# A two-block transformer kernel: the experts' rare branch moved into the last pair, pooling's weights through the chunk ring, sparse attention's keys projected first

## The chip, the cores and the metric

The kernel runs on one core of a Trainium2 chip. A core has five engines, each with its own instruction queue: TensorE (PE, matrix products; its weight loads are listed apart as PEld), VectorE (DVE), ScalarE (ACT), GpSimd (POOL) and SyncE (SP, which here only issues DMAs). They wait for one another on semaphores. The metric is the device time of one execution in microseconds, as the median of the runs.

## The reference

The input is x[256, 1024] in float32. The first block modulates and normalises x, mixes tokens by three branches (attention, gated linear attention, a long convolution), and adds a mixture of 16 experts of which each token takes two from one group. The second block has two layers. Each is a feed-forward, a mixer and another feed-forward, all with norms before and after:

```python
def grouped_moe(h, router_w, router_b, w_gate, w_up, w_down):
    scores = sigmoid(h @ router_w)                    # 16 experts in 4 groups
    sel = scores + router_b
    group = argmax(sum of the 2 best sel in each group)
    idx = top_k(sel inside the group, 2); w = scores[idx] / sum
    for e in range(16):                               # gates: w, or 0
        out += gates[:, e] * ((silu(h @ w_gate[e]) * (h @ w_up[e])) @ w_down[e])

def second_block(x, g, ...):
    for i in range(2):
        x = x + 0.5 * rms_norm(swiglu(rms_norm(x, g[i, 0]), ...), g[i, 1])
        h = rms_norm(x, g[i, 2])
        m = pool_mixer(h) if i == 0 else nsa_mixer(h)
        x = x + rms_norm(m, g[i, 3])
        x = x + 0.5 * rms_norm(swiglu(rms_norm(x, g[i, 4]), ...), g[i, 5])

def pool_mixer(h, w_grp, b_grp, scale):   # 4 channel groups, windows 2, 4, 8, 16
    d = trailing mean over the window - h             # per group
    return (d @ w_grp[g] + b_grp[g]) * scale

def nsa_mixer(h, ...):
    q, k_c, v_c, k_s, v_s, k_w, v_w, gate = split(h @ w_in)
    # compressed keys and values: blocks of 32 tokens through silu(z @ w1) @ w2
    o = sig(gate)[0] * o_compressed + sig(gate)[1] * o_selected + sig(gate)[2] * o_window
    return o @ w_o
```

## The kernel before, in words

Activations stay in on-chip memory, 256 tokens as two tiles `t` of 128 rows. Weights are streamed from memory in chunks of up to 1 MB, requested by SP (L120) into a ring of buffers `wr`; a request waits until the buffer's last reader is done. A float32 weight is split into a rounded part `wh` (ACT, L158) and a rest `wl` (DVE, L159), and a product is made of three passes of matmuls (L169, L171, L173).

*Router and experts* (`moe`). Logits (L992), the norm's sums (L229, L232), scores per token by a small transposing product (L1009), sigmoid, then a chain of small DVE instructions picks group and experts (L1038 to L1064), while PE transposes the tokens (L1027). The tokens are split into `th` and `tl` by ACT (L1031, L1032) and POOL (L1033). `places` writes a 0/1 matrix `put` that gathers up to 64 tokens (`CAP`) of four experts at a time into `xg` by a product (L1092). `fill` (L222) is a matmul without a use for its result. Experts go in eight pairs of 12 chunks each. `first(q)` makes gate and up of pair q (L1138), in its middle the hidden part of the pair before is finished; `second` and `finish` of the pair before (L1184, L1185) follow. The chunk ring has 13 buffers here. If an expert has more than 64 tokens, a branch (L1217) computes the overflow expert by expert; in this input none has, and each engine jumps over some 1500 rows of its program. The branch stands behind the last pair.

*Second block* (`Second`). `ffn` streams 22 + 12 chunks, `project` makes the output, `add` normalises it and adds it to x, one token tile after the other; `after` transposes the next input. `E.ahead` splits the next feed-forward's first chunk early, by ACT (L137) and POOL (L138).

*Pooling* (`pool`). The weights come through the ring, the 1 MB of `band` (the windows' means as matrices), the bias and the scale by POOL's own requests when the stage begins (L84, L1734). For each tile: products (L1745), a scaled copy `v` by ACT (L1747), bias (L1752) and bands (L1754), a multiplication by `scale` (L1756), output.

*Sparse attention* (`nsa`). The columns are projected in the order k_c, v_c, q, k_s, k_w, gate, each 128 columns by three passes. `query` and `key` rotate (L1820, L1822 to L1824) and split by ACT and DVE. `compress` makes the compressed keys and values in steps between the projections. The gates take a sigmoid (L1940) and a transpose (L1945). Then `compressed(t)` makes the scores and probabilities of the compressed keys (L1956 to L1974), and 24 units of `scores` (L1991, L1995, L1997), `softmax` (L2004 to L2011) and `values` (L2022 to L2042) follow, the values two steps behind the scores.

The order on each engine is set by a scheduler that follows the order of the code and its dependences; `issue_after` holds an instruction behind another one.

Of the kernel before, what the change touches and what calls it, by code (L numbers as in the profile page):

```python
# [17 lines left out]
D = 1024  # L18
# [19 lines left out]
class Env:  # L38


    def __init__(self, ctx, tc, W):
        self.ctx = ctx
        self.begun = None
        self.rings = []
        self.beside = ExitStack()
# [56 lines left out]
    @contextmanager  # L102
    def ring(self, name, n):

        with self.pool(name) as p:
            yield p, n

    @contextmanager
    def more_ring(self, n):

        with self.ring("ringmore", n) as r:
            self.rings = [r, *self.kept]
            self.wn = (2048, *self.wn[1:])
            self.turn = 0
            yield
        self.rings = self.kept[:1]
# [6 lines left out]
    def load(self, src, n, eng=None):  # L123

        places = [r for r in self.rings for _ in range(r[1])]
# [3 lines left out]
    def ahead(self, src, n):  # L129
# [4 lines left out]
        with self.tc.high_priority():  # L134
            for i in range(0, n, 512):
                j = slice(i, i + 512)
                ins = self.nc.scalar.activation(hi[:, j], raw[:, j], AF.Copy).ins  # L137
                self.nc.gpsimd.tensor_sub(lo[:, j], raw[:, j], hi[:, j].bitcast(F32))  # L138
        return (hi, lo), ins
# [17 lines left out]
    def split(self, hi, lo, src, eng=None):  # L157
        self.nc.scalar.activation(hi, src, AF.Copy)  # L158
        (eng or self.nc.vector).tensor_sub(lo, src, hi.bitcast(F32))  # L159
# [182 lines left out]
def packs(np, x):  # L342
# [60 lines left out]
    d["rows"] = np.stack([np.broadcast_to(r, (128, 1024)) for r in (g[0, 1], g[0, 3], g[0, 5], g[1, 1], g[1, 3], g[1, 5], x["pool_scale_2"].reshape(1024))])  # L403
    d["pool_b"] = x["pool_b_2"].reshape(1, 1024)
# [5 lines left out]
    cols = np.concatenate([k_c, v_c, q, k_s, k_w, gate, np.zeros((1024, 208), np.float32)], 1)  # L410
# [523 lines left out]
class Chunks:  # L934
# [25 lines left out]

    def take(self):
        return self.got.pop(0) if self.got else self.E.load(next(self.todo), 2048)


def moe(E, W, VI, mc, router, tiles, chunks, xT):
# [18 lines left out]
    def scaled():  # L984

        for k in tiles:
# [5 lines left out]
            mm = PE.matmul(lg[32 * j : 32 * j + 32, :T], rw[:, k], xa[:, k], start=k < 4, stop=k >= 4)  # L992
            if k == KD - 1:
                E.fill(mm.ins, 6)
# [5 lines left out]
    more = es.enter_context(ExitStack())  # L1000
    more.enter_context(E.more_ring(6))
# [6 lines left out]
    for t in range(2):  # L1008
        PE.matmul(lt[:, 16 * t : 16 * t + 16], ls[:, 128 * t : 128 * t + 128], E.sel[:, :16], start=True, stop=True)  # L1009
# [12 lines left out]
    V.tensor_tensor(sel, scores, rb.unsqueeze(1).to_broadcast([128, 2, 16]), OP.add)  # L1022
    for c in range(2):
# [446 lines left out]
class Second:  # L1470
# [94 lines left out]
    def project(self, units, xs, kt, up, after, behind=(), between=None):  # L1565
# [5 lines left out]
        def product(t, w, h, k0, n):  # L1571
# [4 lines left out]
            if k0 + n == kt:  # L1576
                self.out_half(t, h, bank[h, t], self.rows)
                if h:
                    self.add(t, up, after)
# [560 lines left out]
```

## Time and profile before

| | |
|---|---|
| runs | 1717.15 us median of 3 (1712.97 to 1720.77) |
| profiled execution | 1721.04 us, span 1719.3 us, mean granted clock 0.975 |
| busy share of the span | PE 96%, DVE 58%, ACT 45%, POOL 8% |
| DMA | 343.39 MB, mean 200 GB/s over the span |

The busy share is a mean over stages. The windows of the trace give, for a stretch, the busy time of each engine, the TensorE clock that was granted (1.00 is 2.4 GHz, 0.50 is 1.2 GHz) and the DMA share. The timeline lists instructions by start; in brackets stands how long the engine had been idle and what ended that.

### The profile page before, as it was taken

To read this page: it belongs to the slowest core of one execution; us is meant where nothing else is said; L and a number is where in the kernel's file an instruction comes from. 1 tells how busy PE (TensorE), PEld (TensorE's weight loads), DVE (VectorE), ACT (ScalarE), POOL (GpSimd) and SP (SyncE) were. 2 spreads that over 40 slices of the span, in tenths; PEclk is the share of its full clock that TensorE was granted. 3 is DMA by queue.
4 is the path that set the end of the run, shared out by engine and by line. 5 is a ranking of instruction groups with operands and counts; after the bars stand their busy time and mean duration, and the time that the engine had idled before them with its cause. 6 is when DMAs were issued, how large, how long until landed. Compare 5 with 4: busy or idle time off the path is not lost.

```text
span 1719.3 us, 24121 instructions
## 1 busy us (share of the span) xinstructions
PE 1651.5 (96%) x9266; PEld 1286.0 (75%) x9266; DVE 998.1 (58%) x2034; ACT 775.6 (45%) x1616; POOL 145.4 (8%) x149
## 2 busy tenths in 40 slices
PE   6999898899989999989999999999999998999998
PEld 3777787799975444358888688888888897788886
DVE  4635869786552323156654666547555686885544
ACT  3533344365441001045544555436554575865442
POOL 1001215111120000020000000000000022300000
PEclk8999998999999999999999899999999998999999
DMA  9454353137537999956454454555455351065450
GB/s 361 165 185 164 126 169 124 62 99 296 182 145 309 426 425 426 426 227 225 171 188 167 176 190 165 187 193 205 176 182 184 137 198 58 22 257 200 169 190 33
DMA packets 60380, 343.39 MB, mean 200 GB/s; under 512 B 7329, under 2 KB 8161, under 8 KB 28769
## 3 DMA queue, kind: packets, MB, share of 16 engines
q1 hardware_dynamic: 57680, 333.29, 52.0%
q0 software_dynamic: 1776, 6.56, 1.1%
q10 hardware_dynamic: 800, 1.92, 0.3%
q8 instruction: 75, 1.23, 0.3%
q14 instruction: 49, 0.39, 0.1%
HBM read 340.69 MB, written 1.05 MB: 199 GB/s over the span
## 4 chain that ended last, share of the span: by engine, by line
PE 53%; DVE 1%; ACT 1%; DMA 0%; POOL 0%; issue 0%; DVEq 0%; POOLq 0%; ACTq 0%
PE mm L169 16%; PE mm L171 15%; PE mm L173 15%; PE mx L1658 1%; PE mx L1995 1%; PE mx L1507 1%; PE acc L2042 1%; PE mm L2022 1%; PE mm L1754 0%; DMA c_pool_b<-in_pool_b_dram 0%; PE mm L1752 0%; PE mm L1745 0%; PE acc L2031 0%; PE mx L1820 0%; PE acc L2035 0%
## 5 line engine op out<-in xcount | busy, mean ns | idle before, releaser
L159 DVE TENSOR_TENSOR wl<-wr,wh 128x512 fp32r<-128x512 f32 x768 | 498.4, 700 | 237.9 <-ACT wh L158 224.5
L158 ACT ACTIVATE wh<-wr 128x512 fp32r<-128x512 f32 x768 | 428.6, 622 | 307.2 <-PE mm L173 183.1
L169 PE MATMUL mm<-wh,xh 128*128 128x512 f32 (+1 forms) x752 | 204.0, 393 | 0.0
L173 PE MATMUL mm<-wh,xl 128*128 128x512 f32 (+1 forms) x752 | 198.6, 386 | 0.0
L171 PE MATMUL mm<-wl,xh 128*128 128x512 f32 (+1 forms) x752 | 198.2, 386 | 0.0
L173 PEld LDWEIGHTS mm<-wh,xl 128*128 128x128 f32 x752 | 139.1, 188 | 28.7
L171 PEld LDWEIGHTS mm<-wl,xh 128*128 128x128 f32 x752 | 139.1, 188 | 28.6
L169 PEld LDWEIGHTS mm<-wh,xh 128*128 128x128 f32 x752 | 136.1, 188 | 26.1 <-ACT xh L1519 0.4
L1138 PE MATMUL mm<-wr,xg 128*64 128x512 f32 x512 | 124.9, 596 | 0.0
L171 PE MATMUL mm<-wl,hidh 128*128 128x512 f32 x352 | 98.6, 396 | 0.0
L173 PE MATMUL mm<-wh,hidl 128*128 128x512 f32 x352 | 98.0, 396 | 0.0
L169 PE MATMUL mm<-wh,hidh 128*128 128x512 f32 x352 | 97.7, 395 | 0.0
L1650 DVE SCALAR_TENSOR_TENSOR L<-mm,r,L 128x256 f32<-128x256 f32 x88 | 42.5, 483 | 92.8 <-ACT L L1649 90.3
L1649 ACT ACTIVATE L<-mm,r 128x256 f32<-128x256 f32 x88 | 41.8, 475 | 117.5 <-PE mm L173 115.1
L1138 PEld LDWEIGHTS mm<-wr,xg 128*64 128x64 f32 x512 | 37.4, 137 | 67.3 <-issue 64.6
L173 PEld LDWEIGHTS mm<-wh,hidl 128*128 128x128 f32 x352 | 66.1, 188 | 15.8
L171 PEld LDWEIGHTS mm<-wl,hidh 128*128 128x128 f32 x352 | 65.9, 188 | 15.9
L169 PEld LDWEIGHTS mm<-wh,hidh 128*128 128x128 f32 x352 | 65.8, 188 | 15.6
L169 PE MATMUL mm<-hh,wh 128*128 128x256 f32 x480 | 75.1, 295 | 0.0
L173 PE MATMUL mm<-hh,wl 128*128 128x256 f32 x480 | 71.5, 288 | 0.0
L169 PEld LDWEIGHTS mm<-hh,wh 128*128 128x128 f32 x480 | 65.3, 195 | 7.7 <-issue 3.3
L171 PE MATMUL mm<-hl,wh 128*128 128x256 f32 x480 | 70.6, 287 | 0.0
(589 smaller groups left out, 2370.7 us busy)
## 6 DMA issues: line engine op xcount, KB each, us to landing
wr<-in_ffn_in_dram SPq DMA_DIRECT2D x88, 1024.0 KB, 4.8
wr<-in_moe_in_dram SPq DMA_DIRECT2D x64, 1024.0 KB, 12.7
wr<-in_ffn_out_dram SPq DMA_DIRECT2D x40, 1024.0 KB, 4.9
wr<-in_moe_out_dram SPq DMA_DIRECT2D x32, 1024.0 KB, 15.1
wr<-in_w_in_f_dram SPq DMA_DIRECT2D x55, 512.0 KB, 4.1
wr<-in_w_mod_dram SPq DMA_DIRECT2D x48, 512.0 KB, 6.1
wr<-in_nsa_in_f_dram SPq DMA_DIRECT2D x8, 1024.0 KB, 4.7
wr<-in_w_br_att_dram SPq DMA_DIRECT2D x8, 512.0 KB, 3.2
```

The source lines that it names most:

```text
L158: self.nc.scalar.activation(hi, src, AF.Copy)
L159: (eng or self.nc.vector).tensor_sub(lo, src, hi.bitcast(F32))
L169: nc.tensor.matmul(ps, lhs[0][k], rhs[0][k], start=first and k == 0, stop=False)
L171: nc.tensor.matmul(ps, lhs[0][k], rhs[1][k], start=False, stop=False)
L173: mm = nc.tensor.matmul(ps, lhs[1][k], rhs[0][k], start=False, stop=last and k == kt - 1)
L1138: PE.matmul(ps[s], x[:, s], w, start=start, stop=stop)
L1507: E.nc.tensor.transpose(tp[:, 128 * j : 128 * j + 128], self.x[:, t, c : c + 128], E.ident)
L1649: A(s, ps[:, :T], AF.Silu, scale=r)
L1650: V.scalar_tensor_tensor(h, ps[:, T:], r, s, OP.mult, OP.mult)
L1658: PE.transpose(tp[:, 256 * j + 128 * t : 256 * j + 128 * t + 128], hs[n, t][:, 128 * j : 128 * j + 128], E.ident)
L1995: PE.matmul(dst, qs[:, h // 2, h % 2, q], part[:, h // 4, :, : n // 2], start=t == 1 and i == 0, stop=t == 0 and i == 1 and j == 1)
L2022: PE.transpose(tp[:, 128 * j : 128 * j + 128], probs(u)[:, 128 * j : 128 * j + 128], E.ident)
```

## The change

Four places are rewritten.

1. *Router.* The six `fill` matmuls move behind the small transposing product. `th` is written by ACT straight from the transposes in PSUM, `tl` by DVE from there, two instructions behind the chosen mask (`rest_of(0, chosen)`), two behind the first `put`. POOL's subtractions go.
2. *Experts.* The ring has 16 buffers (7 + 2 on top of the kept 7); `xg` has one buffer instead of two. The branch stands in the last pair, after `first(7)`, once all chunks are requested (`chunks.fetch(8)`). The next feed-forward's first chunk is split behind the last pair's own split, and three more of its chunks are requested ahead (`E.queued`).
3. *Pooling.* Weights, rows and band come through the ring; the scale is folded into the weights and the bias by DVE; the bias is one product of one row and 512 columns per bank; the first tile's products and bands come before the feed-forward's add of the second tile (`half`). The next feed-forward's first three chunks are split behind that add (`behind`).
4. *Sparse attention.* Column order k_c, v_c, k_s, k_w, gate, q. The gate is 1 / (1 + exp(-z)) from the transposed values. Two units' scores come before the last query's rotation and the compressed scores; the compressed values' product moves to the end of each group of six units.

```diff
-    more.enter_context(E.more_ring(6))
+    E.more_ring(upper.enter_context(E.ring("ringtop", 2, "right")), more.enter_context(E.ring("ringmore", 7)))
...
-        PE.matmul(lt[:, 16 * t : 16 * t + 16], ls[:, 128 * t : 128 * t + 128], E.sel[:, :16], start=True, stop=True)
+        mm = PE.matmul(lt[:, 16 * t : 16 * t + 16], ls[:, 128 * t : 128 * t + 128], E.sel[:, :16], start=True, stop=True)
+    E.fill(mm.ins, 6)
...
             with E.tc.issue_after(scored):
-                A(h, tp, AF.Copy, scale=rt[:, t : t + 1])
-            nc.scalar.copy(th[:, t, q], h)
-            G.tensor_sub(tl[:, t, q], h, th[:, t, q].bitcast(F32))
+                A(th[:, t, 512 * c : 512 * c + 512], tp, AF.Copy, scale=rt[:, t : t + 1])
+
+    def rest_of(c, after):
+
+        with E.tc.issue_after(after.ins):
+            for t in range(2):
+                q = slice(512 * c, 512 * c + 512)
+                V.scalar_tensor_tensor(tl[:, t, q], turned[c, t], rt[:, t : t + 1], th[:, t, q].bitcast(F32), OP.mult, OP.subtract)
...
-        xg = gp.t([128, KD, n], "xg", 2)
+        xg = gp.t([128, KD, n], "xg")
...
         ps = first(xg[:, :, 128 * (q % 2) : 128 * (q % 2) + 128], two, lambda: next(late, None))
+        if q == 7:
+
+            chunks.fetch(8)
+            far = "far"
+            beyond()
+            far = ""
...
-    *_, last = late
-    E.fill(last, 4)
+
+    upper.close()
+    E.rings = E.kept[:1]
+    begun = E.ahead(W["ffn_in"][0, 0], 2048, done)
+    E.queued = [E.load(W["ffn_in"][0, u], 2048) for u in range(1, 4)]
+    for _ in late:
+        pass
     more.close()
...
-            band = E.const("pool_band", p)
-            b = E.const("pool_b", p)
-            scale = p.t([128, D], "scale")
-            nc.gpsimd.dma_start(scale, W["rows"][6])
+        w = E.load(W["pool_w"], 2048)
+        rows = E.load(W["pool_rows"], 2048)
+        band = E.load(W["pool_band"], 2048).rearrange("a (i g t) -> a i g t", i=2, g=4)
...
-            return tuple([a[:, 512 * k : 512 * k + 512] for k in range(4)] for a in E.wsplit(src[u], 2048))
+            return tuple([a[:, 512 * k : 512 * k + 512] for k in range(4)] for a in E.wsplit(src[u], 2048, behind=behind if u < 3 else ()))
...
-    cols = np.concatenate([k_c, v_c, q, k_s, k_w, gate, np.zeros((1024, 208), np.float32)], 1)
+    cols = np.concatenate([k_c, v_c, k_s, k_w, gate, np.zeros((1024, 208), np.float32), q], 1)
...
+                    A(g2, tp[:, :96], AF.Exp, scale=-1.0)
+                    V.tensor_scalar(g2, g2, 1.0, None, OP.add)
+                    V.reciprocal(g2, g2)
...
+            begin()
+            begin()
+            query(3)
             next(steps[0])
             next(steps[1])
-            next(steps[0])
-            begin()
-            begin()
```

PE around the branch, before: the last pair's `finish` (L1184, L1185), the fill, the branch, and behind its body the next feed-forward (L1674).

```order
L1184 MATMUL mx_6662<-back_6525,xa_6629 128x256
L1185 MATMUL mx_6662<-back_6525,xa_6629 128x256
L222 MATMUL mx_6666<-identr_73 128x512 x4
L1216 TENSOR_LOAD mosti_5425
L1217 COMPARE_AND_BRANCH
```

```order
L1217 UNCONDITIONAL_BRANCH x2
L229 MATMUL mx_11417<-ones_63,eps_69 128x2
L1674 MATMUL mm_11343<-hi_6677,xh_11319 128x512
L1674 MATMUL mm_11344<-hi_6677,xh_11319 128x512
L1674 MATMUL mm_11343<-lo_6678,xh_11319 128x512
```

The same engine now, ahead of the body and behind it (L1157 is the experts' product, L1141 and L1143 belong to `back`).

```order
L1157 MATMUL mm_6456<-wr_6503,xg_6214 64x512
L1157 MATMUL mm_6456<-wr_6505,xg_6214 64x512
L1218 TENSOR_LOAD mosti_5420
L1220 COMPARE_AND_BRANCH
L1141 MATMUL mx_6551<-c_start_61,putfar_6548 128x128 x2
```

```order
L1220 UNCONDITIONAL_BRANCH x2
L1141 MATMUL mx_11154<-c_start_61,put_6211 128x128 x2
L1143 MATMUL mx_11154<-r_812_5412,put_6211 128x2 x2
L1157 MATMUL mx_11164<-wr_6515,L_1039_6489 64x512
L1157 MATMUL mx_11164<-wr_6517,L_1039_6489 64x512
```

The branch has moved from between `finish` of the last pair and the next stage to between `first(7)` and `back(7)` with `second(6)`.

DVE at the pooling, before: the norm of the feed-forward's second tile from the output half (L1563) to its add (L1551), with the next feed-forward's weight splits (L159) between its steps.

```order
L1563 TENSOR_TENSOR xT_12368<-mm_12599,row_11450 128x512
L1498 TENSOR_SCALAR m_2270_12840<-ss_11322 128x1
L159 TENSOR_TENSOR wl_13143<-wr_13141,wh_13144 128x512
L196 TENSOR_SCALAR ny_2271_12842<-m_2270_12840 128x1
L159 TENSOR_TENSOR wl_13143<-wr_13141,wh_13144 128x512
L197 TENSOR_TENSOR nt_2272_12843<-ny_2271_12842 128x1
L159 TENSOR_TENSOR wl_13246<-wr_13244,wh_13247 128x512
L198 SCALAR_TENSOR_TENSOR nt_2272_12843<-nt_2272_12843,m_2270_12840 128x1
L159 TENSOR_TENSOR wl_13246<-wr_13244,wh_13247 128x512
L199 SCALAR_TENSOR_TENSOR nu_2273_12844<-nt_2272_12843 128x1
L159 TENSOR_TENSOR wl_13246<-wr_13244,wh_13247 128x512
L200 SCALAR_TENSOR_TENSOR nt_2272_12843<-nt_2272_12843 128x1
```

The same now (L1593 output half, L1581 add, L158 weight split).

```order
L1593 TENSOR_TENSOR xT_12359<-mm_12590,row_11445 128x512
L1528 TENSOR_SCALAR m_2273_12862<-ss_11319 128x1
L195 TENSOR_SCALAR ny_2274_12864<-m_2273_12862 128x1
L196 TENSOR_TENSOR nt_2275_12865<-ny_2274_12864 128x1
L197 SCALAR_TENSOR_TENSOR nt_2275_12865<-nt_2275_12865,m_2273_12862 128x1
L198 SCALAR_TENSOR_TENSOR nu_2276_12866<-nt_2275_12865 128x1
L199 SCALAR_TENSOR_TENSOR nt_2275_12865<-nt_2275_12865 128x1
L200 SCALAR_TENSOR_TENSOR nu_2276_12866<-nu_2276_12866,ny_2274_12864 128x1
L202 SCALAR_TENSOR_TENSOR rf_11323<-nt_2275_12865,nu_2276_12866 128x1
L1581 SCALAR_TENSOR_TENSOR x_11318<-xT_12359,rf_11323,x_11318 128x512 x2
L158 TENSOR_TENSOR wl_13094<-wr_13092,wh_13095 128x512 x3
```

Between the output half and the add no split is left; the first one stands behind the add.

PE at the start of the sparse attention, before: the last projection (L173, the gates), a rotation, the gates' transposes (L1945), the compressed scores (L1956, L1958), their transposes (L1974), and then the first unit's scores.

```order
L173 MATMUL mm_17082<-xh_11319,wl_17076 128x256 x8
L1820 MATMUL mx_17111<-L_2860_16990,c_nsa_rot_13092 128x512
L1945 MATMUL mx_17126<-c_start_61,L_2873_17107 128x48 x2
L1956 MATMUL mx_17134<-r_cmp_mask_13108,identr_73 128x256
L1958 MATMUL mx_17134<-kc_16425,xT_12368 128x32 x8
L1956 MATMUL mx_17154<-r_cmp_mask_13108,identr_73 128x256
L1958 MATMUL mx_17154<-kc_16425,xT_12368 128x32 x8
L1974 MATMUL mx_17174<-c_start_61,c_r_17152 128x128 x2
L1991 MATMUL mx_17178<-r_causal_13106,identr_73 128x512
```

The same engine now, from the second unit's scores (L2035) on: the last rotation (L1860), the compressed scores (L1996, L1998), and the transposes of the first two units' probabilities (L2062), with the compressed ones (L2014) behind the values (L2073).

```order
L2035 MATMUL mx_17110<-kh_16404,qs_16399 128x256
L2035 MATMUL mx_17110<-kl_16405,qs_16399 128x256
L1860 MATMUL mx_17126<-xT_12359,c_nsa_rot_13067 128x512
L1996 MATMUL mx_17138<-r_cmp_mask_13083,identr_73 128x256
L1998 MATMUL mx_17138<-kc_16400,xT_12359 128x32 x8
L1996 MATMUL mx_17158<-r_cmp_mask_13083,identr_73 128x256
L1998 MATMUL mx_17158<-kc_16400,xT_12359 128x32 x8
L2062 MATMUL mm_17231<-c_start_61,two_17094 128x128 x4
L2062 MATMUL mm_17238<-c_start_61,two_17094 128x128 x4
```

Scores of two units have moved ahead of the compressed scores, and the gates' transposes away from the end of the projections.

## Rows read from the trace of the kernel before

**Rows 1.** windows: length, busy PE, loads, DVE, ACT, POOL; clock, DMA share, GB/s

```profile
500.00:520.00 20.00, 13.14 (x74) 10.67 (x73) 10.58 (x40) 5.79 (x12) 4.95 (x4) 0.89 0.77 316
520.00:540.00 20.00, 20.00 (x102) 9.53 (x103) 3.15 (x8) 3.56 (x6) 0.00 (x0) 0.94 0.57 232
560.00:580.00 20.00, 20.00 (x94) 7.44 (x90) 5.39 (x11) 1.79 (x3) 0.00 (x0) 1.00 1.01 425
740.00:760.00 20.00, 16.36 (x68) 9.90 (x65) 7.79 (x18) 8.73 (x19) 7.31 (x7) 0.91 0.32 118
940.00:960.00 20.00, 16.02 (x68) 11.54 (x66) 14.06 (x46) 15.03 (x40) 2.14 (x4) 0.90 0.59 238
960.00:980.00 20.00, 20.00 (x66) 13.45 (x66) 11.47 (x37) 8.18 (x22) 0.04 (x1) 0.76 0.35 113
1440.00:1460.00 20.00, 17.67 (x78) 14.57 (x79) 12.01 (x32) 13.06 (x43) 2.63 (x4) 0.66 0.00 1
```

**Rows 2.** timeline at the router: start, length, engine, line, idle before

```profile
503.74 1.66 PE L222 MATMUL mx<-identr 128*128 128x512 f32 x6
...
510.28 0.16 DVE L1044 TENSOR_TENSOR r<-r 128x8 f32<-128x8 f32 x1
...
510.43 4.95 POOL L1033 TENSOR_TENSOR tl<-L,th 128x512 fp32r<-128x512 f32 x4 [10.46 <-ACT th L1032]
...
510.79 2.17 DVE L1049 SCALAR_TENSOR_TENSOR r<-r,r,cs 128x4 f32<-128x4 f32 x2
...
513.18 0.99 DVE L1051 TENSOR_TENSOR r<-r,r 128x8 f32<-128x8 f32 x1
514.21 1.21 DVE L1064 SCALAR_TENSOR_TENSOR r<-r,r 128x32 f32<-128x32 f32 x1
...
515.57 0.64 PE L1067 MATMUL mx<-r,cs 128*128 128x48 f32 x2 [4.37 <-DVE r L1064]
...
523.94 0.88 DVE L1097 TENSOR_SCALAR xg<-mx,modc 128x256 f32<-128x256 f32 x2 [1.22 <-PE mx L1092]
```

**Rows 3.** DMA issues: KB each, median us from issue to landing

```profile
wr<-in_moe_in_dram SPq DMA_DIRECT2D x64, 1024.0 KB, 12.7
```

**Rows 4.** instructions of line L1217: duration in ns, first and last start

```profile
L1217 SPq EVENT_SEMAPHORE  x8: 17/17/17, 739.6 to 740.1; - x8
L1217 SPq COMPARE_BRANCH  x1: 50/50/50, 734.9 to 734.9; - x1
L1217 ACTq COMPARE_BRANCH  x1: 54/54/54, 746.5 to 746.5; - x1
L1217 ACTq EVENT_SEMAPHORE  x1: 17/17/17, 749.0 to 749.0; - x1
...
L1217 PEldq COMPARE_BRANCH  x1: 3592/3592/3592, 749.9 to 749.9; - x1
```

**Rows 5.** timeline behind the last pair, PE

```profile
753.80 0.35 PE L229 MATMUL mx<-ones,eps 1*128 1x2 f32 x2 [3.30 <-PEq L1217]
```

**Rows 6.** timeline at the pooling

```profile
947.33 0.51 POOL L84 DMA_DIRECT2D c_pool_b<-in_pool_b_dram  x1
...
949.25 0.68 DVE L159 TENSOR_TENSOR wl<-wr,wh 128x512 fp32r<-128x512 f32 x1
...
954.83 0.67 PE L1752 MATMUL mm<-c_pool_b,ones 1*128 1x256 f32 x2 [3.98 <-DMA c_pool_b<-in_pool_b_dram]
```

**Rows 7.** timeline at the start of the sparse attention

```profile
1427.53 0.63 ACT L1893 ACTIVATE qs<-L 128x512 fp32r<-128x512 f32 x1 [4.14 <-POOL L L1824]
...
1440.12 0.32 PE L1945 MATMUL mx<-c_start,L 48*128 48x48 f32 x2 [3.42 <-ACT L L1940]
...
1449.47 0.69 PE L1974 MATMUL mx<-c_start,c_r 128*128 128x128 f32 x2 [1.77 <-POOL c_r L1969]
...
1452.46 0.19 ACT L2007 ACTIVATION_READ_ACCUMULATOR xT<-mx,a_st 128x1 f32 x1
...
1452.56 0.36 ACT L2007 ACTIVATE xT<-mx,a_st 128x128 f32<-128x128 f32 x1
```

More of the change, by code (lines that the diff above doesn't have):

```diff
@@ L1140, in first @@
     def first(xg, take, between):
[L1142 removed]
+        ps = [E.mx() if far else E.mm() for _ in range(2)]
         for j in range(2):
@@ L1195, in rest, with beyond, one @@
         yield finish(second(hid, two), bk)
+    def beyond():
+        count = nc.values_load(mosti[0:1, 0:1], min_val=0, max_val=256)
+        rings, E.rings = E.rings, E.kept[1:]
+        with E.tc.If(count > CAP):
+            for e in range(16):
+                for i in range(2):
+                    own = p.t([128, 2, 1], "own")
+                    V.tensor_scalar(own, place[:, :, e : e + 1], -float(CAP + 128 * i), None, OP.add)
+                    put, _ = places(own, 1, 128)
+                    slot, bk = back(put, gates[:, :, e : e + 1])
+                    srcs = iter([W["moe_in"][e, j] for j in range(4)] + [W["moe_out"][e, c] for c in range(2)])
+                    def one():
+                        return [E.load(next(srcs), 2048)]
+                    ps = first(gather(put), one, lambda: None)
+                    finish(second(hidden(ps, slot), one), bk)
+        E.rings = rings
     xg = gather(put)
@@ L1205, in moe @@
             xg = gather(put)
-        next(late, None)
+        done = next(late, None)
         late = rest(ps, slot, bk)
-    *_, last = late
-    E.fill(last, 4)
-    more.close()
-    begun, ins = E.ahead(W["ffn_in"][0, 0], 2048)
-    with E.tc.issue_after(ins):
-        count = nc.values_load(mosti[0:1, 0:1], min_val=0, max_val=256)
-    with E.tc.If(count > CAP):
-        for e in range(16):
-            for i in range(2):
-                far = p.t([128, 2, 1], "far")
-                V.tensor_scalar(far, place[:, :, e : e + 1], -float(CAP + 128 * i), None, OP.add)
-                put, _ = places(far, 1, 128)
-                slot, bk = back(put, gates[:, :, e : e + 1])
-                srcs = iter([W["moe_in"][e, j] for j in range(4)] + [W["moe_out"][e, c] for c in range(2)])
-                def one():
-                    return [E.load(next(srcs), 2048)]
-                ps = first(gather(put), one, lambda: None)
-                finish(second(hidden(ps, slot), one), bk)
+    upper.close()
[4 more added lines that the diff above has]
+        pass
+    more.close()
     es.close()
@@ L1563, in out_half, with project @@
         E.nc.vector.tensor_mul(self.f[:, q : q + 512], ps, row[:, 512 * h : 512 * h + 512])
-    def project(self, units, xs, kt, up, after, behind=(), between=None):
+    def project(self, units, xs, kt, up, after, behind=(), between=None, half=iter(())):
         E = self.E
@@ L1593, in project @@
             for w, (h, k0, n, src) in zip(ws, units[-3:]):
-                product(t, w, h, k0, n)
+                self.behind = product(t, w, h, k0, n)
+            if t:
+                next(half, None)
+            self.add(t, up, after)
+        self.last_added = self.added
+        next(half, None)
     def gained(self, g):
```

213 lines of the change are left out of this document (111 added, 102 removed).

## Prediction

> **What bounds the kernel now.** I read the windows first (busy time and granted clock), then the timeline around each window that is not full, then the branch's line and the DMA issues. In the middle of the experts TensorE (PE) is busy for all of its 20.00 us at granted clock 1.00, while the DMA share is 1.01 and VectorE (DVE) and ScalarE (ACT) do little [rows 1]: the kernel is bound by PE's own work, and time is to be had only where PE idles or runs at its lower level. Those places are few. At the lower of the two levels, 1.2 GHz, a 20 us window with clock c holds (1 - c) x 40 us. That makes 4.4 + 2.4 = 6.8 us before the first expert, 3.6 us behind the last, 4.0 + 9.6 = 13.6 us in the pooling, and 13.6 us at the start of the sparse attention [rows 1]; each time PE had idled for 3.3 to 4.4 us just before the clock fell [rows 2, 5, 6, 7]. Work that runs there takes double, so half of such a stretch is lost beside the idle time itself. The change works at exactly these four places, and I sum over them.
>
> The sum is made on the profiled execution, 1721.04 us (span 1719.3). It lies 3.9 above the median of 1717.15 and at the upper edge of the three runs; I subtract the sum from the median.
>
> **Router, before the first expert: -8.8.** The six filling matmuls stand between the last logits and the norm's sums and take 1.66 us; in the new order they stand behind the small transposes that feed the scores, off the path. Then DVE picks the experts by a chain of small instructions. One costs 0.16 us (L1044), but from 510.43 GpSimd (POOL) runs its four subtractions, 4.95 us, and in that stretch L1049's two take 2.17, L1051 0.99 and L1064 1.21 [rows 2]. At 0.16 each these four instructions would be 0.64 instead of 4.37: -3.7. The subtractions go; in their place DVE reads the transposes from PSUM, two instructions behind the chosen mask and two behind the first `put`. The first two, at the price of a 512-column DVE instruction (0.68, L159 [rows 6]), lie beside PE's place counting; the last two lie ahead of the gather's second half. PE's idle time of 4.37 before L1067 [rows 2] falls to under 1, and I expect no fall of the clock: half of 6.8, -3.4. Together -1.7 - 3.7 - 3.4 = -8.8. If the clock falls anyway, -5; if the chain shortens further, -10.5.
>
> **The gathered tokens in one buffer instead of two: +2.2.** For the third and fifth gather the evacuations must wait until the old tokens' last expert product is read, and the second half of the pair before waits behind them on PE. One pair of evacuations is 0.88 [rows 2]; with its matmuls I take 1.1, twice. Bounds 0 and +4.
>
> **16 chunk buffers instead of 13: 0.** A chunk lands a median 12.7 us after its issue [rows 3], because the queue is full; PE does not wait, its window is full [rows 1]. More buffers only deepen the queue.
>
> **The branch for crowded experts, and the last pair: +1.9.** Before, its skip stands at the very end. PE's branch takes 3592 ns [rows 4], PE idles 3.30 us until L229 [rows 5], four filling matmuls stand ahead of it (1.1, at the price of the router's six), and the 3.6 us at the lower level cost 1.8: -6.2 if all of it goes. It comes back in the last pair, between the first and the second half, where PE has no other work that may pass it. SyncE (SP) is the only engine that took the branch while a 1 MB chunk was in flight: 734.9 to 739.6, 4.7 us, against 2.5 for ACT (746.5 to 749.0) on a quiet queue [rows 4]. At the new place chunks are in flight, so I price PE's idle time by SP's row, 4.7, plus half of 6.8 us at the lower level as behind the router's gap of similar length, 3.4: +8.1. Net 8.1 - 6.2 = +1.9. The next layer's first part, split by ACT and POOL, now waits for the last pair's split; three more of its chunks are requested ahead, which covers it, so it costs nothing. Bounds: 3.3 idle and a clock that stays up give -3; one chunk's whole queue time of 12.7 and 13.6 us at the lower level (6.8) give +13.
>
> [...]
>
> **Pooling: -10.8.** Before, a 4 KB bias is requested by POOL at 947.33, behind a 1 MB band and beside SP's chunks, and PE waits 3.98 us for it [rows 6]; then come 13.6 us at the lower level, half of them lost: 6.8. Now weights, band and bias come through the ring, issued long before, and the bands of the first token tile stand ahead of that wait's place. -4.0 - 6.8 = -10.8. What is late next? The norm behind the feed-forward's second tile. In the old order five splits of DVE at 0.68 us [rows 6] stand between its steps; in the new order they stand behind the add, which takes 3.4 us off it and brings the transposes under the cover of the first tile's products and bands. Those splits are then needed right after: the first weights' lie beside the band matmuls, but the ring holds the pooling's three chunks, and the second weights' chunk takes over a buffer only when the first's split is done. Bounds: -4 if the clock still falls, -14 if the norm chain shortens PE's path as well.
>
> **Sparse attention: -5.4.** Before, PE idles 3.42 us for the sigmoid of the gates and 1.77 for the compressed probabilities, and of the 13.6 us at the lower level, 1.77 of them idle, half of the other 11.8, 5.9, is lost [rows 1, 7]: 11.1 in all. The keys are now projected first, and the gates are ready while queries are still projected, so both waits go. A new one comes: behind the last projection PE has two units' scores, a rotation and the compressed scores, and then transposes that need both units' softmax. Behind the scores ACT has eight exponentials of 0.36 + 0.19 and eight copies of queries at 0.63 [rows 7], 4.4 + 5.0 = 9.4 us, and DVE's scaling behind them; PE's scores and compressed products run beside that and cover it from the front. I take 4.0 us of idle time, a little under half of the 9.4, and half of 3.4 us at the lower level behind it, 1.7: -11.1 + 5.7 = -5.4. Bounds -11.1 and +2 (the wait in one piece, with 13.6 us at the lower level).
>
> **Sum:** -8.8 + 2.2 + 1.9 - 10.8 - 5.4 = -20.9. On the profiled execution 1700.1; on the median 1696.3, so 1696.
>
> **Rivals.** (1) *The gaps close, the clock stays low.* At attention and pooling the idle time goes but a shorter one still drops the clock for as long as before: 6.8 comes back at the pooling and 5.1 (6.8 - 1.7) at the attention, of which I count three quarters, 9: 1705. For it: a gap of 3.30 dropped it for 3.6 us and one of 3.42 for 13.6 [rows 1, 5, 7], so length says little. Against: at the pooling the new order leaves no wait of that length.
> (2) *The ring starves the next feed-forward.* Three chunks of the pooling hold their buffers until its end, and the parts of the second and third weights come late: one chunk's landing behind others, up to 8 us: 1704. Against: SP issues well ahead, and the queue behind the experts is not full [rows 1].
> (3) *The jump waits in the chunk queue.* Before, PE took it on a quiet queue; SP's 4.7 was under a single chunk. If the fetch of the code behind the jump is served behind the chunks, each wait is 12.7 us [rows 3]. One wait, with 6.8 lost to the clock: +19.5 instead of +8.1, 1708. Three in a row (the branch and the two unconditional ones that the order shows) with the same loss: 38.1 + 6.8 instead of 8.1, 36.8 more: 1733, slower than before. It decides from 29 us more than I priced, three waits. Against: the two unconditional ones belong to the body and are jumped over; and SP's row is 2.2 above ACT's, not a whole chunk. [...]
>
> **How the numbers follow.** The forecast gets 0.62, rival 1 0.15, rival 2 0.08, rival 3 0.15 (0.10 with one wait, 0.05 slower than before). No more than about 0.5%, 8.6 us, can be told from no change here. Around the forecast, the terms' bounds that add independently (2, 2, 6, 4 and 5) give some 9 us, 1687 to 1705; to hold 8 in 10 with the rivals I go up to 1710 and down to 1684, where the jump is cheap and the attention's whole loss goes. Faster: forecast and rivals 1 and 2 nearly whole, half of one wait: 0.85. Same: 0.10. Slower: 0.05.
>
> **What would show it.** Right: POOL without subtractions, and durations like L1044's through the router's chain; no wait of PE on a DMA in the pooling and clock 1.00 there; the branch's idle time at 4 to 6 us inside the last pair. Wrong: an idle time over 10 us at the branch; PE waiting for ACT's split of the second weights behind the pooling; the transposes of the attention's first two units waiting over 5 us, or low clock for over 10 us in any of the four windows.

## The result

The changed kernel takes 1706.17 us (median of 6 runs, 1702.32 to 1709.46) against 1717.41 for the kernel before (6 runs, 1712.97 to 1720.77): ratio 0.9935, 95% interval 0.9921 to 0.9949, 11.2 us less. Forecast were 20.9 us less; 1706 lies inside the range of 1684 to 1710. The profiled execution of the changed kernel took 1709.46 us (span 1707.3).

Kernels with the same code up to the router reach it at different times: its last logits start at 503.2 us in the trace of before, at 504.1 in that of after, and between 499.9 (e4) and 504.2 (e3) in the others. So I compare lengths between fixed instructions of PE, in us; each is worked out from two start or end times in one profiled execution:

| from ... to | before | after | difference | forecast |
|---|---|---|---|---|
| last logits ... first expert product (router) | 20.63 | 11.64 | -9.0 | -8.8 |
| ... last back product (experts) | 225.58 | 233.70 | +8.1 | +10.3 (buffer 2.2, branch 8.1) |
| ... pooling's first product | 197.83 | 192.69 | -5.1 | -6.2 |
| ... next feed-forward's first product (pooling) | 30.62 | 20.36 | -10.3 | -10.8 |
| ... start of the sparse attention | 387.51 | 388.18 | +0.7 | 0 |
| ... its last value product | 136.23 | 138.15 | **+1.9** | **-5.4** |
| ... end | 210.29 | 210.35 | +0.1 | 0 |

Together -13.6 in these two executions, where -20.9 were forecast. (As wholes they differ by 11.6: after reached the router 0.9 later and took 1.2 longer outside the rows of this table.) The 7.3 that are missing are the attention's row; the other rows miss by up to 2.2 each way and cancel. The 2.4 from 13.6 to the medians' 11.2 are within the runs' scatter and the ratio's interval (-8.8 to -13.6).

The windows of the changed kernel, as in [rows 1]:

```profile
500.00:520.00 20.00, 18.34 (x115) 13.34 (x116) 11.23 (x48) 6.70 (x13) 0.00 (x0) 1.00 0.90 366
560.00:580.00 20.00, 20.00 (x98) 7.87 (x100) 3.84 (x10) 0.60 (x1) 0.00 (x0) 1.00 1.01 420
720.00:740.00 20.00, 15.22 (x66) 6.58 (x68) 6.51 (x15) 3.27 (x6) 4.99 (x4) 0.91 0.58 233
940.00:960.00 20.00, 20.00 (x82) 14.78 (x81) 14.12 (x51) 12.53 (x36) 0.56 (x1) 0.91 0.31 101
960.00:980.00 20.00, 19.70 (x85) 14.70 (x84) 17.62 (x50) 13.79 (x37) 0.00 (x0) 1.00 0.84 328
1420.00:1440.00 20.00, 18.30 (x108) 14.20 (x107) 12.72 (x27) 11.92 (x33) 7.01 (x6) 0.83 0.01 2
1440.00:1460.00 20.00, 17.55 (x124) 12.87 (x126) 14.99 (x44) 15.34 (x68) 8.73 (x9) 1.00 0.00 1
```

The lower level takes 3.6 us behind the branch, 3.6 in the pooling, 6.8 in the attention and nothing at the router, where before it took 6.8 at the router, 3.6, 13.6 and 13.6.

The router's timeline, which answers [rows 2]:

```profile
505.67 1.64 PE L221 MATMUL mx<-identr 128*128 128x512 f32 x6
...
508.61 0.36 DVE L1061 SCALAR_TENSOR_TENSOR r<-r,r,cs 128x4 f32<-128x4 f32 x2
...
509.19 0.17 DVE L1063 TENSOR_TENSOR r<-r,r 128x8 f32<-128x8 f32 x1
509.39 0.19 DVE L1076 SCALAR_TENSOR_TENSOR r<-r,r 128x32 f32<-128x32 f32 x1
509.50 1.40 DVE L1045 SCALAR_TENSOR_TENSOR tl<-mm,rtok,th 128x512 fp32r<-128x512 f32 x2
...
509.64 0.42 PE L1080 MATMUL mx<-r,cs 128*128 128x48 f32 x2 [0.28 <-DVE r L1076]
...
511.61 0.69 PE L1110 MATMUL mx<-put,th 128*128 128x256 f32 x3 [1.13 <-DVE put L1095]
```

The four DVE instructions that took 4.37 us beside POOL's subtractions take 0.36 + 0.17 + 0.19 = 0.72, and PE's wait for the last of them is 0.28 instead of 4.37. What is left is a wait of 1.13 for `put`.

The branch, which answers [rows 4, 5]: first its instructions, then the timeline of PE and SP behind it.

```profile
L1220 SPq EVENT_SEMAPHORE  x8: 17/17/17, 710.3 to 724.4; - x8
...
L1220 SPq COMPARE_BRANCH  x1: 50/50/50, 703.8 to 703.8; - x1
...
L1220 ACTq COMPARE_BRANCH  x1: 54/54/54, 713.5 to 713.5; - x1
L1220 PEldq COMPARE_BRANCH  x1: 6252/6252/6252, 715.1 to 715.1; - x1
L1220 ACTq EVENT_SEMAPHORE  x1: 17/17/17, 718.8 to 718.8; - x1
```

```profile
721.71 0.41 PE L1141 MATMUL mx<-c_start,put 128*128 128x128 f32 x2 [1.87 <-PEq L1220]
...
724.74 3.62 PE L1157 MATMUL mx<-wr,L 128*64 128x512 f32 x8 [1.71 <-issue]
724.84 3.09 SPq L117 DMA_DIRECT2D wr<-in_ffn_in_dram  x4
```

The jump takes PE 6252 ns instead of 3592, of which 1.87 us show as idle time, since the products in front of it are still running. SP's eight semaphore instructions come one by one with the landings of chunks: the first at 710.3, when the chunk requested at 693.9 lands (16.3 us later), the last at 724.4, behind the landing of the last one (requested at 702.8, 21.4 us). Only then are the next chunks requested, at 724.84, and only at 724.74 does PE's next expert product start, 1.71 us after it could. Its row names no releaser, so that SP's late semaphores held it is inferred from the times.

The pooling, which answers [rows 6], PE:

```profile
951.13 3.90 PE L1785 MATMUL mm<-wr,xg 128*128 128x256 f32 x12
...
954.87 0.60 PE L1537 MATMUL mx<-c_start,x 128*128 128x128 f32 x4
...
956.61 1.89 PE L1792 MATMUL mm<-wl,wr 128*128 128x256 f32 x8
```

No wait of PE on a DMA is left there. The attention comes with the reasons below.

### The profile page after: what moved, and what is told of

Its sections match the earlier page's. It is cut to its first block, busy times and chain, and to the rows that moved or that the text cites. A ratio compares the mean times of both kernels' runs of the same rounds, so it can differ in the third digit from the quotient of the medians.

```text
span 1707.3 us, 24075 instructions
## 1 busy us (share of the span) xinstructions
PE 1646.5 (96%) x9254; PEld 1276.8 (75%) x9254; DVE 1000.3 (59%) x2039; ACT 770.7 (45%) x1611; POOL 139.0 (8%) x141
## 4 chain that ended last, share of the span: by engine, by line
PE 52%; DVE 2%; ACT 2%; issue 1%; POOL 0%; DVEq 0%; ACTq 0%; POOLq 0%
PE mm L172 15%; PE mm L170 15%; PE mm L168 15%; PE mx L1693 1%; PE mx L1157 1%; DVE wl L158 1%; PE acc L2080 1%; PE mm L2062 1%; PE mx L1537 1%; ACT wh L157 1%; PE mm L1785 0%; PE mx L2035 0%; PE acc L2073 0%; PE mm L1792 0%; ACT xT L2047 0%
## 5 line engine op out<-in xcount | busy, mean ns | idle before, releaser
L158 DVE TENSOR_TENSOR wl<-wr,wh 128x512 fp32r<-128x512 f32 x768 | 501.8, 705 | 230.2 <-ACT wh L157 216.5
L1157 PE MATMUL mm<-wr,xg 128*64 128x512 f32 x512 | 123.8, 596 | 0.0
L1157 PEld LDWEIGHTS mm<-wr,xg 128*64 128x64 f32 x512 | 37.2, 137 | 67.6 <-issue 63.5
```

The costliest lines, as they stand in the source:

```text
L1157: PE.matmul(ps[s], x[:, s], w, start=start, stop=stop)
```

## The experiments

Twelve kernels, each timed beside the kernel before on the same chip, in 5 rounds (e6, e7 and e8 in 3), and profiled once. "Stage" is a row of the table above.

**The old attention in the changed kernel (e1).** The method `nsa` and the order of its columns are those of before.

```diff
-cols = np.concatenate([k_c, v_c, k_s, k_w, gate, np.zeros((1024, 208), np.float32), q], 1)
+cols = np.concatenate([k_c, v_c, q, k_s, k_w, gate, np.zeros((1024, 208), np.float32)], 1)
... (def nsa as in the kernel before)
```

> The changed kernel with the sparse attention and its column order of the kernel before; router, experts, branch and pooling as changed. Theory (the attention's rewrite is the term that failed: from the last norm ahead of it to its last product it takes 138.2 us in the changed kernel, 136.2 before): about 2 us less than the changed kernel's 1706.2, 1702 to 1706. Rival (the rewrite gains the 5.4 us that were forecast and the loss sits elsewhere): 5 us more, about 1711.

Measured: 1705.88 us, ratio 0.992 (0.9903 to 0.9936), as good as the changed kernel. The stage takes 138.24 with the old code and 138.15 with the new, where the theory had 136.2 for the old. So in these surroundings the rewrite is worth nothing. **The other way round (e11)**, the kernel before with only the attention of the change (its `nsa` and its columns):

> The kernel before with only the sparse attention of the change (keys projected first, its new start). The prediction's term: -5.4 us, attention stage 136.2 to 130.8, median 1712. Theory after the earlier runs (the two waits that go come back as a new wait for the compressed softmax, a split in the weights' ring ahead of the projections, and query copies beside the units): stage 137.5-138.5, median 1718-1720, no gain.

Measured: 1721.78 us, ratio 1.0026 (1.0011 to 1.0041): 0.3% slower. The stage rises from 136.23 to 139.52. The term's sign was wrong, and the waits come with the code, wherever it stands.

**The compression's split out of the weights' ring (e2).** In the changed kernel the compressed input `z` is split into a buffer of the ring `wh` that the projections' weights pass through. Here its halves lie in the keys' tiles, which are written later.

```diff
-zh, zl = (... E.wp.t([128, 2048], "wh", E.wn[2], FR)))
+zh, zl = (a.rearrange("a g w t -> a (g w t)")[:, :1024].rearrange("a (j n) -> a j n", j=16) for a in (kh, kl))
...
-                if w:
-                    key(0, raws[0])
-                else:
+                if not w:
                     second = compress(1)
                 next(first)
                 next(second)
+            key(0, raws[0])
```

> The changed kernel, but the compressed blocks' two parts zh, zl lie in the (not yet written) key tiles instead of in the ring of weight parts wh; the first key's rotation follows the second compression's product. Theory (ACT's splits of the weights come late because a part's buffer is taken from them): the three waits of PE on splits in the attention's projections (0.58, 0.44 and 0.55 us, with two small ones 1.9 in all) go, 1.5 to 3 us less than the changed kernel, 1703 to 1705. Rival (ACT and DVE are late because the compressions' copies and additions are in the way, whichever buffer they use): the waits stay, within 1 us of 1706.

Measured: 1702.12 us, ratio 0.9897 (0.988 to 0.9915); the stage falls by 4.3 to 133.83. PE among the projections, in the changed kernel and then in this one:

```profile
1366.80 1.27 PE L168 MATMUL mm<-xh,wh 128*128 128x256 f32 x8 [0.58 <-ACT wh L157]
...
1372.86 1.51 PE L168 MATMUL mm<-wh,wh 128*64 128x256 f32 x8
...
1377.77 0.45 PE L170 MATMUL mm<-wl,wh 128*64 128x256 f32 x2 [0.44 <-DVE wl L158]
...
1381.75 1.53 PE L168 MATMUL mm<-xh,wh 128*128 128x256 f32 x8 [0.55 <-ACT wh L157]
```

```profile
1366.38 1.12 PE L168 MATMUL mm<-xh,wh 128*128 128x256 f32 x8
...
1369.26 1.09 PE L168 MATMUL mm<-wh,kh 128*64 128x256 f32 x8
...
1374.86 1.12 PE L168 MATMUL mm<-xh,wh 128*128 128x256 f32 x8
```

In the changed kernel PE waits for weight splits (0.58, 0.44, 0.55 and two of 0.15), and some groups of eight matmuls take 1.27 to 1.53 instead of 1.09 to 1.12. The first scores of the stage start 74.6 us after its start there, in e3, e10 and e11 as well, and 70.7 in the three kernels with `z` elsewhere (e2, e5, e12): 3.9 us, twice the 1.9 of the waits that the theory counted. The edit also moves the first key's rotation, which was not tried alone.

**The compressed probabilities later (e3).** Their small tile gets two buffers, their transposes come two steps later.

```diff
-                st = ap.t([128, 2, 16], "c_st")
+                st = ap.t([128, 2, 16], "c_st", 2)
...
-                if n < 2:
-                    next(steps[n])
+                if 2 <= n < 4:
+                    next(steps[n - 2])
```

> The changed kernel, but the compressed probabilities have two buffers for their statistics and their transposes stand two steps later, behind the first values. Theory (PE's wait of 2.47 us for the second tile's probabilities is a wait in a wrong place, nothing else needs them so early, and the fall of the clock at that place follows from PE's waits there): that wait goes and with it some of the 6.8 us at the lower level, 2.5 to 5 us less than the changed kernel, 1701 to 1704. Rival (ACT's exponentials set the pace of the first units, the wait only moves to the next transposes): within 1 us, 1705 to 1707.

Measured: 1703.28 us, ratio 0.9901 (0.9882 to 0.992); stage 134.57. The wait for POOL in the changed kernel, then here, and this kernel's window:

```profile
1442.11 0.44 PE L2014 MATMUL mx<-c_start,c_r 128*128 128x128 f32 x2 [2.47 <-POOL c_r L2009]
```

```profile
1439.02 0.44 PE L2014 MATMUL mx<-c_start,c_r 128*128 128x128 f32 x2 [0.99 <-POOL c_r L2009]
```

```profile
1420.00:1440.00 20.00, 16.95 (x118) 14.52 (x117) 14.70 (x36) 14.98 (x45) 7.33 (x7) 1.00 0.01 3
```

The wait falls from 2.47 to 0.99, but others come: the stage's idle time is 5.9 instead of 6.6. The granted clock stays at 1.00, where the changed kernel had 0.83 (its window 1420 above); that is nearly all of the stage's 3.6 us. That the edit keeps the clock up is not shown: in e5 and e12, which have it too, the clock falls at this place. **Both edits (e5)**:

> The changed kernel with both earlier edits of the attention: the compressed blocks' parts in the key tiles, and the compressed probabilities' transposes two steps later with two buffers for their statistics. Alone they took the attention from 138.15 us to 133.83 and 134.57. Theory (two different losses, waits on weight splits among the projections, and a wait at the first units with the clock's fall behind it): they add, 130 to 131 us in the attention and about 1698 in all. Rival (both only keep the clock up, by removing a wait shortly before it falls): no more than the better one, 133 to 134 us, 1702.

Measured: 1701.08 us, ratio 0.9901 (0.9883 to 0.9918); stage 133.08, where 130 to 131 was the sum and 133 to 134 the rival. Idle time falls to 3.5, but the clock is 0.83 again. e12 below has the same attention code and takes 131.16, with 0.91 there, so one profiled execution doesn't decide between the two.

**The branch left out, after and before (e4, e7).** In e4 the changed kernel loses the three lines that call it; in e7 the kernel before loses it at its old place.

```diff
             chunks.fetch(8)
-            far = "far"
-            beyond()
-            far = ""
```

> The changed kernel without the branch: the overflow of crowded experts is left out (none has more than 64 tokens in this input). Theory (the branch in the last pair costs PE 1.87 us of idle time for the jump, 1.71 for a chunk's semaphore that SP brings up only when the last chunk in flight has landed, and half of the 3.6 us at the lower level, 1.8): 5.4 us less than the changed kernel, 1700 to 1702. Rival (it is nearly free there, since the pair is bound by the chunks' landing): under 2 us less, 1704 to 1706.

> The kernel before without the branch: the overflow of crowded experts is left out. Theory (at the old place the branch costs PE's 3.3 us and half of the 3.6 us at the lower level, and nothing else stands behind it): 5 us less, about 1712. Rival (as in the changed kernel without the branch, where PE then waited 3.9 us for POOL's squares ahead of the norm's sums, another wait takes the place): 0 to 2 us less, 1715 to 1717.

Measured: e4 1702.27 us, ratio 0.9899 (0.9882 to 0.9917), experts' stage 227.21 instead of 233.70; but the stretch behind them rises from 192.69 to 196.88. e7 1721.44, ratio 1.0017 (1.0007 to 1.0027): nothing gained, even 0.2% lost. PE, POOL and DVE behind the last pair of e7, and POOL's same three instructions in the kernel before:

```profile
764.18 1.01 PE L232 MATMUL mx<-mean,L 128*128 128x1 f32 x4 [4.30 <-POOL L L1600]
```

```profile
753.12 11.01 POOL L1600 TENSOR_TENSOR L<-L,L 128x512 f32<-128x512 f32 x3 [2.69 <-issue]
```

```profile
753.01 7.30 DVE L159 TENSOR_TENSOR wl<-wr,wh 128x512 fp32r<-128x512 f32 x12
```

```profile
758.12 4.35 POOL L1616 TENSOR_TENSOR L<-L,L 128x512 f32<-128x512 f32 x3 [5.46 <-ACT L L1614]
```

Without the jump PE meets the next wait, for POOL's squares of the next norm: 4.30 instead of 0.40 us in before (3.92 in e4). The squares start earlier, 5.7 us behind the experts instead of 8.7, and end later, at 16.7 instead of 13.1. The first of the three takes 8.33 us beside DVE's twelve weight splits in a row and ends 1.1 us behind them; the other two take 1.27 each, and the three in before 1.29 to 1.61, where DVE's first such split starts only at 760.60. In e4 the first takes 7.16 beside ten splits. **The branch behind the last pair of the changed kernel (e9)**, all else kept: the three lines stand after the last `finish`.

> The changed kernel with the overflow branch behind the whole last pair again, as in the kernel before; 16 chunk buffers, the ring and all else stay. Theory (the jump costs PE 6.5 us inside the last pair because nothing may pass it, while at the end PE waits 3.9 to 4.3 us for POOL's squares anyway): the experts' stage falls from 233.7 to about 227.2 us, the stretch from the last back product to the pooling's first product rises from 192.7 to 197-199, so 0 to 2 us less in all, median 1702-1706. Rival (the place is indifferent, the jump costs its 6 us wherever it stands, on top of the squares): the second stretch rises to 203 or more, median 1709 or more.

Measured: 1707.84 us, ratio 0.9947 (0.9929 to 0.9965), 1.7 us above the changed kernel and within both scatters. The stretch behind the experts takes 200.39, between theory (197 to 199) and rival (203 or more).

```profile
745.90 0.55 PE L228 MATMUL mx<-ones,eps 1*128 1x2 f32 x2 [4.13 <-PEq L1220]
```

```profile
740.00:760.00 20.00, 15.87 (x61) 12.66 (x60) 9.91 (x23) 10.60 (x22) 9.10 (x8) 0.83 0.58 215
```

From the first expert product to the pooling: 424.09 without a branch, 426.39 with it in the pair, 427.70 with it at the end. It costs 2.3 or 3.6 us net by these traces, so the place decides little.

**The bias ahead of the band, in the kernel before (e6).**

```diff
-            band = E.const("pool_band", p)
             b = E.const("pool_b", p)
+            band = E.const("pool_band", p)
```

> The kernel before, with the two requests of the pooling's constants in the other order: the 4 KB bias ahead of the 1 MB band, on the same queue. Theory (the wait is one for that queue: the band is needed 2 us after the bias and lands no earlier, so the wait moves to it): the pooling from its first product to the next feed-forward stays at 29 to 31 us, 1716 to 1718. Rival (the bias alone was late): the 4 us and part of the time at the lower level go, 20 to 25 us, 1708 to 1713.

Measured: 1715.26 us, ratio 0.9999 (0.9987 to 1.0011). The wait only changes its name:

```profile
951.49 0.70 PE L1754 MATMUL mm<-v,c_pool_band 128*128 128x256 f32 x2 [2.56 <-DMA c_pool_band<-in_pool_band_dram]
```

The stage is 27.29 instead of 30.62, between theory and rival, with 3.6 us at the lower level instead of 13.6. That is no gain of the order: e8, with the requests as in before, has 27.41 and 6.8 us at the lower level. So the order of two requests at the stage's start doesn't help; by the rows above, in which PE waits for no DMA, the request long before does. No run has that part of the change alone.

**The router's rest by DVE, alone, in the kernel before (e8).**

```diff
-            nc.scalar.copy(th[:, t, q], h)
-            G.tensor_sub(tl[:, t, q], h, th[:, t, q].bitcast(F32))
+                A(th[:, t, 512 * c : 512 * c + 512], tp, AF.Copy, scale=rt[:, t : t + 1])
...
+                V.scalar_tensor_tensor(tl[:, t, q], turned[c, t], rt[:, t : t + 1], th[:, t, q].bitcast(F32), OP.mult, OP.subtract)
...
+    rest_of(0, chosen.ins)
...
```

> The kernel before with one part of the router's edit: th from PSUM by ACT, tl by DVE behind the chosen mask and the first put, no subtraction by POOL; the filling matmuls stay where they were. Theory (DVE's small instructions were slow because POOL's subtractions ran beside them: 4.37 us for four instead of 0.64): DVE's chain is 3 to 4 us shorter, and the time from the last logits to the first expert falls from 20.6 to 14 to 17 us, 1711 to 1714 in all. Rival (the chain was waiting for something else, and two added DVE instructions of 0.7 us stand in it): 19 to 21 us.

Measured: 1713.34 us, ratio 0.9971 (0.9959 to 0.9984); stage 16.20 instead of 20.63, half of the router's gain. Of the 4.6 us to the changed kernel's 11.64, the filling matmuls are 1.7 by their length and the lower level 1.5 to 1.8 (3.6 us of it here, none there); the rest is not taken apart.

**Without the hold on the splits behind the add (e10).**

```diff
-... E.wsplit(src[u], 2048, behind=behind if u < 3 else ()))
+... E.wsplit(src[u], 2048))
```

> The changed kernel without the hold that keeps the first three weight splits of the feed-forward behind the add. The prediction's view (five splits of 0.68 us between the norm's steps delay the second token tile's norm by 3.4 us): the stage from the pooling's first product or the following feed-forward starts lose up to 3.4 us, and the pooling's stretch goes from 20.4 to 22-24 us. Rival (the bands of the first token tile cover the norm, so the hold is worth nothing or costs because the splits come late): 19-20.5 us and a median within 1 us of the changed kernel's 1706.

Measured: 1706.29 us, ratio 0.994 (0.9919 to 0.9961), as the changed kernel; pooling 19.06. The hold is worth nothing, as the rival has it; the 1.3 us that the stage is shorter go with a clock of 1.00 at 940 to 960 (0.91 in the changed kernel). With the hold, e1, e2, e3 and e5 also have 1.00 there and 19.05 to 19.06.

**Three edits together (e12)**: those of e5 and e9.

> The changed kernel with three edits together: the compression's split out of the weights' ring with the compressed softmax later, and the branch behind the last pair. Theory that the places are independent: attention stage 133.1 instead of 138.2, plus what the branch's place gives alone (0 to 2): 1698-1701. Rival (the branch at the end only moves the wait): 1701-1703, as with the attention's edits alone.

Measured: 1699.28 us, ratio 0.9899 (0.9879 to 0.9919). Its median is the lowest here, 18.7 us below that of the kernel before beside it, but by their ratios e2, e3, e4, e5 and e12 can't be told apart (0.9897 to 0.9901); so the branch's place adds nothing that these runs show.

## Why the prediction was right, and where it failed

The time lies in the range because router and pooling, -19.6 of the forecast, measured -19.3 and mostly in the way that was forecast. **The failed step** is the attention's term, "-11.1 + 5.7 = -5.4". It measured +1.9. The windows' clocks take it apart. Taking off half of the time at the lower level, as the prediction did, leaves an estimate of the stage at full clock. (Work there took 1.8 times as long, not quite double: in before, pairs of 512-column products (L1674) follow every 0.85 us from 754.24 to 756.80, at a clock of 0.50 (1.2 columns per ns), and every 0.46 to 0.47 from 758.23 to 759.63, at 1.00. The same code at two clocks checks the half: 3.6 us at the lower level cost 1.5 in the router and 1.3 in the pooling, 3.2 us cost 1.9 between e12 and e5; in the last pair, where PE waits, 3.2 us more cost 0.3 between after and e1.)

| kernel | stage | at the lower level | at full clock |
|---|---|---|---|
| before | 136.2 | 13.6 | 129.4 |
| e1, old code in the changed kernel | 138.2 | 16.8 | 129.8 |
| after | 138.2 | 6.8 | 134.8 |
| e10 | 137.7 | 6.8 | 134.3 |
| e11, new code in the kernel before | 139.5 | 10.4 | 134.3 |
| e3 | 134.6 | 0 | 134.6 |
| e2, `z` out of the ring | 133.8 | 6.8 | 130.4 |
| e5, `z` out of the ring | 133.1 | 6.8 | 129.7 |
| e12, `z` out of the ring | 131.2 | 3.6 | 129.4 |

The clock's part was about right: -5.9 + 1.7 = -4.2 forecast, -3.4 measured. The new waits among the first units hit in sum, 4.0 us forecast and 0.62 + 0.42 + 0.31 + 2.47 measured, but by luck: the transposes that were to wait for both units' softmax wait 0.42 and 0.31, and the largest is the wait for the compressed probabilities, which was counted as gone (1.77 before, 2.47 now). At full clock the forecast comes to 129.4 - 5.2 + 4.0 = 128.2, and 134.8 was measured: 6.6 us are missing from the sum. Most of them, 4.4 (after to e2) to 4.9 (e3 to e5), go when `z` leaves the ring, 3.9 of that ahead of the first scores: they lie in the projections, which I left at no cost, since I looked for waits behind them only. There the compression's split took a buffer of the weights' ring and stood on ACT and DVE ahead of the splits that PE needs next. ACT's splits in the changed kernel, where the 1024-column form is that of `z`:

```profile
1365.17 3.66 ACT L157 ACTIVATE wh<-wr 128x1024 fp32r<-128x1024 f32 x6 [0.76 <-DVE wr L1891]
...
1380.12 1.58 ACT L157 ACTIVATE wh<-wr 128x1024 fp32r<-128x1024 f32 x2 [4.17 <-DVE wr L1891]
```

ACT waits 0.76 us there for DVE to finish `z`, and 4.17 the second time, with the weights queued behind it; PE's waits of 0.58 and 0.55 follow. The line stood in the diff of the two kernels (`zh, zl` in `"wh"`). Without it, at full clock, the new order is as fast as the old (129.4 to 130.4 against 129.4 and 129.8) and no faster, though PE idles less: 3.9 us in e2, 3.5 in e5 and 2.9 in e12, against 5.9 in before. So its products take some 3 us longer there, and this rest of the missing term stays open.

**Router**: -9.0 for -8.8; the mechanism is the one forecast (POOL's subtractions gone, 4.37 to 0.28). That the clock stayed at 1.00, as forecast, is in part luck: it also did in e4, e5, e10 and e12, but with the same code it fell for 3.6 us in e1, e2, e3 and e9 (stage 13.1).

**Single buffer**: forecast twice 1.1; PE waits twice 0.93, at 609.40 (shown) and 668.80.

```profile
609.40 2.83 PE L1157 MATMUL mx<-wr,L 128*64 128x512 f32 x12 [0.93 <-ACT xg L1117]
```

**Branch**: net +1.9 forecast, about +1 measured (experts +8.1 and -5.1 behind them, less 1.9 for the buffer). That the net came near is luck: its two terms did not stand as priced. In the pair the jump costs 6.5 us on the spot (e4), from an idle time of 1.87 + 1.71, 3.6 us at the lower level and what it delays, where 8.1 was forecast; but 4.2 of it come back without the branch, as a wait for POOL's squares. SP's 4.7, by which the idle time was priced, need not be a jump's price alone: its first semaphore instruction at 739.6 came 0.3 us behind the landing of the chunk requested at 733.68 (5.6 us). At the old place taking the branch away gains nothing (e7), for the same reason as in e4, where 6.2 were forecast. The stretch behind the experts fell by 5.1 all the same: the jump is gone from it, and, other than in e4 and e7, little comes in its place. ACT's first work for the next feed-forward, in the kernel before and in the changed one:

```profile
753.68 3.30 ACT L1602 ACTIVATE xh<-xT,c_gain 128x256 fp32r<-128x256 f32 x8 [5.04 <-PEq L1217]
```

```profile
747.56 1.71 ACT L1637 ACTIVATE xh<-xT,c_gain 128x256 fp32r<-128x256 f32 x4 [1.15 <-DVE xT L1205]
```

It starts 4.3 us behind the experts' last product in before, and 1.8 ahead of it now. The squares start 5.0 us behind the experts and end at 11.0, with six splits of DVE beside them (the first square takes 2.58), and PE's wait for them is 0.15 us at 760.45. Why fewer splits fall beside them than in e4 isn't shown. Rival 3 (waits behind the chunks) was true in kind: the jump grew from 3592 to 6252 ns with chunks in flight, and SP was held until 724.4; but PE did not pay a chunk's 12.7 us, and that a fetch of code waited behind the chunks isn't shown. Rival 2 (the next feed-forward starves) did not come: its row differs by 0.7.

**Pooling**: -10.3, or -9.6 with the 0.7 behind it, for -10.8; the reason stands, except for the hold (e10). Both sides depend on the execution, with the clock: the old code took 30.62, 30.63 (e7), 30.31 (e11) and 27.41 (e8), the new one 19.05 to 20.36. **16 buffers**: as forecast nothing; PE is busy for the whole window at 560.

Rival 1 (the gaps close, the clock stays low) holds at neither of its places as written: in the pooling and at the attention the clock fell for a quarter to a half of its former time.

**Open**: when the clock falls. In the pooling of after PE is busy for 20.00 of 20 us at 0.91, and e1, e2, e3 and e5 have 1.00 with the same code there; at the router the same code had 1.00 and 0.91. So a profiled execution with a fall and one without differ by up to some 2 us in a stage, and why e3's attention had none with more idle time than e5's isn't settled. That the projections' 4 to 5 us go with `z` out of the ring is shown by e2, e5 and e12; how they divide between the buffer and the order on ACT was not tried. In e2 both change: two weight splits (1361.88) come ahead of that of `z` (1362.94).

## What to carry to other kernels

When an edit puts work of its own into a ring that feeds the bounding engine, count that work in the step that it now shares, not only in the step that it was meant for: 4 to 5 us were lost in the one part that had seemed untouched. Before counting a wait as gained, find what PE would wait for next without it; here a jump with 3.3 us of idle time behind it was worth nothing by itself, since without it the squares on another engine ran beside a row of weight splits and ended later. And move requests to where the data is idle long before: swapping two requests at the point of need changed only the wait's name.

## What the runs showed of the hardware

A jump over the same code cost more while chunks were landing. PE's took 3592 ns behind the last pair of the kernel before and 3652 there in e9, with DMA shares of 0.08 and 0.17 in those stretches (749.9 to 753.5, 741.9 to 745.6), and 6252 inside the last pair, with 0.91 (715.1 to 721.4). ACT's next instruction came 2.5 us after its compare in before [rows 4] and 5.3 here (713.5 to 718.8). The queues for instructions move 2 packets in the stretch of PE's jump in before and 4 in that here; for which engine, and whether the jump waits for them, isn't shown.

SP, joining behind the skipped branch, was held by transfers in flight: its eight semaphore instructions, which it took within 0.5 us in the kernel before [rows 4], took from 710.3 to 724.4 here, each behind a chunk's landing until the last chunk was there, and it requested nothing in that time.

DVE's 0.16 us instructions had taken up to 1.2 us beside POOL's 512-column subtractions [rows 2]; without them the same ones took 0.17 to 0.19. The other way round, a 512-column square of POOL took 8.33 us (e7) and 7.16 (e4) beside DVE's weight splits in a row, and 1.27 behind them.
